# The attention heads' products in three rounded terms, x loaded a second time, and an opening by three queues

## The chip, the core and the metric

The kernel runs on one core of one Trainium2 chip. A core has five engines with instruction streams of their own: TensorE (PE in the profile, its weight loads PEld), VectorE (DVE), ScalarE (ACT), GpSimd (POOL) and SyncE (SP). DMAs are issued on the queues of SP, ACT and Pool and carried by the core's 16 DMA engines. The metric is the time of one execution on the device in microseconds (us), the median of several runs.

## The reference

One layer of a streaming encoder, all in float32, with S = 256 rows, D = 2048 columns, 16 heads of 128 columns:

```python
h = rms_norm(x, attn_norm)
proj = h @ w_in                      # 2048 x 6152: qa, ka, va, fa, qb, kb, vb
# group A, 8 heads, forgetting attention
qa, ka = rms_norm(heads(qa), q_norm), rms_norm(heads(ka), k_norm)
c = cumsum(log_sigmoid(fa + b_forget))
p = softmax(qa . ka / sqrt(128) + c[t] - c[s], s <= t);        out_a = p @ va
# group B, 8 heads, stick-breaking attention
z = qb . kb / sqrt(128)
log_beta = log_sigmoid(z);  log_1m = where(s < t, log_beta - z, 0)
suffix = reverse_cumsum(log_1m) - log_1m
w = where(s < t, exp(log_beta + suffix), 0);                   out_b = w @ vb
x = x + concat(rms_norm(out_a, out_norm_fox), rms_norm(out_b, out_norm_sb)) @ w_out
# feed-forward: causal convolution of width 3, gate, down projection
u = conv(rms_norm(x, ffn_norm) @ w_up) + conv_b                # 2048 x 11264
x = x + (silu(gate) * val) @ w_down                            # 5632 x 2048
```

## The kernel before

**Numbers in two parts.** The weights come from memory as F32. Each block of weights (a tile `w_raw`, mostly 1 MB) is split into two tiles of the rounded type F32R: ScalarE casts it to `w_hi` (L197), VectorE subtracts to get the rest, `w_lo` (L198). The activations (`hT`, `oT`) are kept in two such parts as well. A large product is then three F32R products that add up in PSUM: high by high, high by low, low by high. `in_three` (L219) does that for `token_major` products with 512 columns; `from_features` (L246, L253) does it where features lie on the partitions, with 512 columns for the high part of the weights and 256 for the low part.

**Order.** The opening (the first projection, one block of q) and the feed-forward part are ordered by hand (`tc.manual_schedule`). Between them a scheduler orders every engine's instructions by priority and dependency. The blocks of weights are loaded on SP's queue and split with a high priority, two blocks ahead (`whi` and `wlo` have two buffers each, `wraw` three). The work of the heads is written as generators, which wait in a queue (`waiting`); after each step of a projection (24 products of 512 columns, or 32 products in `from_features`) `step()` advances the first two of them. PE thus does a head's small products at the boundaries between two steps, and DVE and ACT do what lies between those products while PE works on the next step.

**The heads.** Heads of group A (`fox_head`): the rows of q and k are normed (`fox_rows`) and transposed (`to_heads`) into F32 tiles `qA`, `kA`; `ps_s` holds the scores of 128 and 256 columns (L505, L506), DVE and ACT make the softmax `pr`, PE transposes it (L530), ACT copies it to `pT`, and `ps_o` is the product with `vA` (L536, L537). Heads of group B (`sb_head`): q and k come as features on partitions from `sb_heads`, `ps_z` holds the scores (L576, L577); ACT makes Abs, Exp and Ln, DVE the softplus `sp`, both split it into `sps`, PE adds the sums over the later keys with six F32R products against `ntri` (L595 to L597), ACT takes Exp to get `w`, DVE limits it, and `ps_o` is the product with `vB` (L604, L605). All score products and value products are plain F32 products; the `ntri` products are F32R. `attended` scales the result into `oT` (L331, high and low part) and sums its squares.

**The opening.** `opening()` loads slices of x and of `w_in`, transposes x with the identity (first 128 columns of `cs`), scales it with the columns of `prow` (`attn_norm`) into `hT` (ACT, L140, then DVE's low part, L143), and multiplies (L386). SP's queue starts with x and then `cs`, ACT's with the first half of the first weights, then `prow`, then the second half:

```python
load_x(0, 2)
nc.sync.dma_start(cs[:, :P], cst[:, :P])
load_w(0, nc.scalar, [0])
nc.scalar.dma_start(prow[:KT, :], attn_norm[0].rearrange("(n p) -> n p", p=P))
load_w(0, nc.scalar, [1])
...
keep_busy(17)
columns(ga, prow[:KT, :], KT)
keep_busy(0)
split_w(0)
keep_busy(6)
```

`keep_busy(n)` is n products of a tile of zeros, whose result nobody uses; Pool sets the zeros (L344).

**x and minus_c.** x stays in the tile `x2` (2 MB) from the opening to the output projection, which adds to it (L642). `minus_c`, the gates of group A spread over all partitions, is made through a small tensor in memory, `c_rows`, on Pool's queue.

Of the kernel before, what the change touches and what calls it, by code (L numbers as in the profile page):

```python
# [8 lines left out]
F32 = mybir.dt.float32  # L9
# [5 lines left out]
P = 128  # L15
# [26 lines left out]
def hybrid_layer(  # L42
# [39 lines left out]
    x2 = big.tile([P, NT, D], F32, name="x2")  # L82
# [191 lines left out]
    with ExitStack() as actx:  # L274
# [15 lines left out]
        def to_heads(dst, rows, t, scale):  # L290

            ps = psb.tile([P, 4, P], F32, name="ps_h", tag="t")
            for h in range(4):
                nc.tensor.transpose(ps[:, h, :], rows[:, h * HD : (h + 1) * HD], ident)  # L294
            act.activation(dst[:, :, t * P : (t + 1) * P], ps, AF.Identity, scale=scale)
# [30 lines left out]
        def attended(po, h, g, group):  # L326

            o = oT[group * NH + h]
            act.activation(o[:, 0, :], po, AF.Identity, scale=g[:, h : h + 1])
            dve.scalar_tensor_tensor(  # L330
                o[:, 1, :], po, g[:, h : h + 1], f32(o[:, 0, :]), op0=ALU.mult, op1=ALU.subtract  # L331
            )
            if h == 0:
                act.activation(ssq[group], po, AF.Square)
            else:
                sq = tmp.tile([P, S], F32, name="osq", tag="t1", bufs=3)
                act.activation(sq, po, AF.Square)
                dve.tensor_tensor(ssq[group], ssq[group], sq, op=ALU.add)
# [5 lines left out]
        nc.gpsimd.memset(zeros, 0.0)  # L344
# [8 lines left out]
        def opening():  # L353
# [14 lines left out]
            def split_w(c):  # L368
                hi = whi.tile([P, 2048], F32R, name="w_hi", tag="w_hi")
                lo = wlo.tile([P, 2048], F32R, name="w_lo", tag="w_lo")  # L370
                parts.append([t[:, :1024].rearrange("p (a b) -> p a b", a=2) for t in (hi, lo)])
                for i, n in pairs[c]:
                    cols = slice(i * 512, (i + n) * 512)
                    act.copy(hi[:, cols], raws[c][:, cols])
# [71 lines left out]

        def heads_tile(name):
            return at.tile([P, 4, S], F32, name=name, tag="qk", bufs=4)

        qT0 = heads_tile("qA0")  # L450
# [3 lines left out]
        vA = at.tile([P, NT, WF], F32, name="vA")  # L454
        lf = at.tile([P, NT, NH], F32, name="lf")
        for j in range(3):
            acc = project(2 * WF + 344 * j, 344)
            n = 344 if j < 2 else 336
            for t in range(NT):
                scaled(vA[:, t, 344 * j : 344 * j + n], acc[:, t, :n], t)  # L460
                if j == 2:
                    dve.scalar_tensor_tensor(
                        lf[:, t, :], acc[:, t, 336:344], rstd1[:, t : t + 1], bf,
                        op0=ALU.mult, op1=ALU.add,
                    )


        c_of = at.tile([P, NT, NH], F32, name="c_of")
        minus_c = at.tile([P, NH, S], F32, name="minus_c")
# [3 lines left out]
        def gates():  # L473
# [19 lines left out]
            nc.gpsimd.dma_start(minus_c, c_rows.unsqueeze(0).to_broadcast([P, NH, S]))  # L493

        waiting.append(gates())
        step()

        def fox_head(h, qT, kT, first):
# [4 lines left out]
            q, k = qT[:, h % 4, :], kT[:, h % 4, :]  # L503
            s0, s1 = ps[:, 0, :], ps[:, 1:3, :].rearrange("p a b -> p (a b)")
            nc.tensor.matmul(s0, q[:, :P], k[:, :P], start=True, stop=False)  # L505
            nc.tensor.matmul(s1, q[:, P:], k, start=False, stop=True)  # L506
# [3 lines left out]
            for o, s, t in ((p0, s0, 0), (p1, s1, 1)):  # L510
                dve.scalar_tensor_tensor(
                    o, minus_c[:, h, : (t + 1) * P], c_of[:, t, h : h + 1], s, op0=ALU.add, op1=ALU.add
                )
# [17 lines left out]
            pT = tmp.tile([P, 3, P], F32, name="pT", tag="pT")  # L531
            act.copy(pT, pt)
            yield
            po = psb.tile([P, S], F32, name="ps_o", tag="t")
            hs = slice(h * HD, (h + 1) * HD)
            nc.tensor.matmul(po, vA[:, 0, hs], pT[:, 0:2, :].rearrange("p a b -> p (a b)"), start=True, stop=False)  # L536
            nc.tensor.matmul(po[:, P:], vA[:, 1, hs], pT[:, 2, :], start=False, stop=True)  # L537
            attended(po, h, g_fox, 0)

        for half in range(2):  # L540
            if half:
                qT = heads_tile("qA1")
# [4 lines left out]
            kT = heads_tile(f"kA{half}")  # L547
# [12 lines left out]
        def sb_heads(c0, scale, name):  # L560
            dst = heads_tile(name)
# [6 lines left out]
            return dst  # L568

        def sb_head(h, qT, kT, v):  # L570
            q, k = qT[:, h % 4, :], kT[:, h % 4, :]
# [4 lines left out]
            mm(z0, k[:, :P], q, start=True, stop=False)  # L576
            mm(z1, k[:, P:], q[:, P:], start=False, stop=True)  # L577
# [20 lines left out]
            w = tmp.tile([P, 3, P], F32, name="w", tag="pT")  # L598
            act.activation(w, ps, AF.Exp)
            dve.tensor_tensor(w[:, 0::2, :], w[:, 0::2, :], limit2, op=ALU.min)  # L600
            yield
            po = psb.tile([P, S], F32, name="ps_o", tag="t")
            hs = slice((h % 4) * HD, (h % 4 + 1) * HD)
            mm(po, v[:, 0, hs], w[:, 0:2, :].rearrange("p a b -> p (a b)"), start=True, stop=False)  # L604
            mm(po[:, P:], v[:, 1, hs], w[:, 2, :], start=False, stop=True)  # L605
            attended(po, h, g_sb, 1)

        for half in range(2):
            qT = sb_heads(B0 + 512 * half, R1q, f"qB{half}")
            kT = sb_heads(B0 + WF + 512 * half, R1, f"kB{half}")  # L610
            v = at.tile([P, NT, 512], F32, name=f"vB{half}", tag="vB", bufs=1)
            acc = project(B0 + 2 * WF + 512 * half, 512)
            for t in range(NT):
                scaled(v[:, t, :], acc[:, t, :], t)
# [11 lines left out]
        for group in range(2):  # L626
# [378 lines left out]
```

## Time and profile before

| | |
|---|---|
| median of 3 runs | 1116.93 us (1116.54 to 1117.72) |
| profiled execution, its own time | 1115.63 us |
| span of its instructions | 1113.7 us |
| busy PE (products) | 1106.9 us, 99% |
| busy PEld (weight loads) | 957.9 us, 86% |
| busy DVE | 862.7 us, 77% |
| busy ACT | 692.7 us, 62% |
| busy POOL | 27.2 us, 2% |
| TensorE's granted clock | 1.00 over the whole span |
| DMA | 231.34 MB, mean 208 GB/s |

Busy times are of each engine alone, so they overlap. Weight loads lie beside the products: a product's weights are loaded while the one before is under way. A row of the chain names the work that the last instruction can be followed back to. In rows of single instructions or groups of neighbours, the first two numbers are start and length in us, then engine, line, operation, output <- inputs, shape and count, and in brackets idle time before it and what ended that.

### The profile page before, as it was taken

The page shows a single profiled execution, that of the slowest core. Times are in us where ns is not written, and L with a number is a line of the kernel's source. Part 1 is how long each engine was busy: PE and PEld are TensorE (multiplying, and loading weights), DVE is VectorE, ACT ScalarE, POOL GpSimd, SP SyncE. Part 2 cuts the span into 40 slices and gives each one's busy share as a digit, 9 for nine tenths or more (in the row PEclk, how much of TensorE's full clock was granted, in tenths as well). Part 3 has the DMA queues.
Part 4 walks back from the last instruction along what each step waited for, and adds up shares of the span by engine and source line. Part 5 has one row for each costly group of instructions (what it writes and reads, how often), then busy time and mean ns, then how long its engine had stood idle before and what let it go on. Part 6 is the DMA issues. An engine that isn't in the chain of part 4 may idle for free.

```text
span 1113.7 us, 14715 instructions
## 1 busy us (share of the span) xinstructions
PE 1106.9 (99%) x5873; PEld 957.9 (86%) x5873; DVE 862.7 (77%) x906; ACT 692.7 (62%) x849; POOL 27.2 (2%) x27
## 2 busy tenths in 40 slices
PE   9999999999999999999999999999999999999998
PEld 7998888888888888888888888888888888888886
DVE  5745666657666677788899898989989899989973
ACT  6544545355565567666777767775777667776751
POOL 0000000000000000000000000000000000000000
PEclk9999999999999999999999999999999999999999
DMA  8676656564445486496869696788859697697941
GB/s 260 213 227 227 190 152 189 155 185 153 152 152 164 137 271 207 126 263 181 259 211 254 208 265 218 227 243 228 248 184 251 219 266 248 193 266 195 297 161 67
DMA packets 172479, 231.34 MB, mean 208 GB/s; under 512 B 4192, under 2 KB 118266, under 8 KB 172282
## 3 DMA queue, kind: packets, MB, share of 16 engines
q1 hardware_dynamic: 162378, 209.93, 58.3%
q0 software_dynamic: 9712, 19.93, 10.2%
q8 instruction: 46, 0.75, 0.3%
q10 hardware_dynamic: 320, 0.53, 0.2%
q14 instruction: 23, 0.19, 0.0%
HBM read 228.28 MB, written 2.11 MB: 207 GB/s over the span
## 4 chain that ended last, share of the span: by engine, by line
PE 98%; DVE 1%; DMA 0%; ACT 0%; issue 0%; SPq 0%; DVEq 0%; ACTq 0%
PE pu L246 33%; PE acc L219 24%; PE pu L253 18%; PE bank_a L219 10%; PE bank_b L219 4%; PE bank_c L219 2%; PE acc L386 2%; PE ps_x L135 1%; DVE w_lo L198 1%; DMA cs<-in_cst_dram 0%; PE ps_z L576 0%; PE ps_o L604 0%; PE ps_s L506 0%; PE ps_o L536 0%; PE ps_h L294 0%; PE ps_p L530 0%
## 5 line engine op out<-in xcount | busy, mean ns | idle before, releaser
L198 DVE TENSOR_TENSOR w_lo<-w_raw,w_hi 128x2048 fp32r<-128x2048 f32 (+2 forms) x200 | 440.1, 2204 | 161.9 <-ACT w_hi L197 156.0
L197 ACT CAST w_hi<-w_raw 128x2048 fp32r<-128x2048 f32 (+2 forms) x200 | 368.1, 1841 | 239.4 <-PE acc L219 91.2
L246 PE MATMUL pu<-hT,w_hi 128*128 128x512 f32 x1664 | 397.6, 391 | 0.0
L246 PEld LDWEIGHTS pu<-hT,w_hi 128*128 128x128 f32 x1664 | 310.1, 188 | 63.2
L253 PEld LDWEIGHTS pu<-hT,w_lo 128*128 128x128 f32 x1664 | 213.6, 191 | 8.2
L253 PE MATMUL pu<-hT,w_lo 128*128 128x256 f32 x1664 | 216.2, 283 | 0.0
L219 PE MATMUL acc<-w_hi,hT 128*128 128x512 f32 (+1 forms) x576 | 126.0, 370 | 0.0
L219 PEld LDWEIGHTS acc<-w_hi,hT 128*128 128x128 f32 x576 | 101.6, 188 | 14.3
L709 ACT ACTIVATE tap<-up,ccol 128x256 f32<-128x256 f32 x176 | 74.6, 495 | 0.0
L198 DVE TENSOR_TENSOR w_lo<-w_sum,w_hi 128x2048 fp32r<-128x2048 f32 (+1 forms) x30 | 62.2, 2073 | 13.4 <-ACT w_hi L197 10.6
L197 ACT CAST w_hi<-w_sum 128x2048 fp32r<-128x2048 f32 (+1 forms) x30 | 51.9, 1731 | 22.8 <-PE pu L246 22.8
L219 PE MATMUL acc<-w_lo,hT 128*128 128x512 f32 (+1 forms) x288 | 64.6, 366 | 0.0
L219 PEld LDWEIGHTS acc<-w_lo,hT 128*128 128x128 f32 x288 | 51.6, 188 | 7.5
L219 PE MATMUL acc<-w_hi,oT 128*128 128x512 f32 x192 | 46.3, 393 | 0.0
L219 PE MATMUL bank_a<-w_hi,g 128*128 128x512 f32 x176 | 44.2, 392 | 0.0
L219 PEld LDWEIGHTS acc<-w_hi,oT 128*128 128x128 f32 x192 | 35.4, 188 | 7.0
L219 PEld LDWEIGHTS bank_a<-w_hi,g 128*128 128x128 f32 x176 | 31.8, 189 | 5.7
L219 PE MATMUL bank_a<-w_hi,s 128*128 128x512 f32 x144 | 36.5, 393 | 0.0
L219 PE MATMUL bank_b<-w_hi,s 128*128 128x512 f32 x144 | 36.4, 392 | 0.0
L714 DVE TENSOR_TENSOR gate<-gate,tap 128x512 f32<-128x512 f32 x44 | 30.3, 688 | 2.3
L714 DVE TENSOR_TENSOR val<-val,tap 128x512 f32<-128x512 f32 x44 | 30.3, 688 | 2.3
L815 POOL DMA_DIRECT2D w_raw<-in_w_down_dram x10 | 12.7, 1270 | 779.6 <-DVE s L761 373.9
(176 smaller groups left out, 1052.1 us busy)
## 6 DMA issues: line engine op xcount, KB each, us to landing
w_raw<-in_w_up_dram SPq DMA_DIRECT2D x88, 1024.0 KB, 5.8
w_raw<-in_w_down_dram SPq DMA_DIRECT2D x40, 1024.0 KB, 5.3
w_raw<-in_w_in_dram SPq DMA_DIRECT2D x36, 1024.0 KB, 5.3
w_raw<-in_w_out_dram SPq DMA_DIRECT2D x16, 1024.0 KB, 5.2
w_raw<-in_w_in_dram SPq DMA_DIRECT2D x12, 688.0 KB, 4.2
w_raw<-in_w_down_dram POOLq DMA_DIRECT2D x8, 1024.0 KB, 12.0
w_sum<-in_w_down_dram POOLq DMA_DIRECT2D x8, 1024.0 KB, 9.0
w_raw<-in_w_down_dram SPq DMA_DIRECT2D x8, 512.0 KB, 4.0
```

The lines of the kernel that those rows point to most:

```text
L135: nc.tensor.transpose(ps[:, j, t * P : (t + 1) * P], xt[t][:, (k + j) * P : (k + j + 1) * P], ident)
L197: act.copy(hi[:, :n], raw[:, :n])
L198: dve.tensor_tensor(lo[:, :n], raw[:, :n], f32(hi[:, :n]), op=ALU.subtract)
L219: nc.tensor.matmul(o, lhs(i, l, t), r[:, i, :], start=starts and j == 0, stop=stops and j == 3 * n - 1, skip_group_check=more,)
L246: nc.tensor.matmul(acc[:, j, :], hi[:, i, j * P : (j + 1) * P], hT[:, k].rearrange("p a b -> p (a b)"), start=k == 0, stop=False,)
L253: nc.tensor.matmul(acc[:, j, S:], lo[:, i, j * P : (j + 1) * P], hT[:, k, 0, :], start=False, stop=k == KT - 1,)
L386: nc.tensor.matmul(acc[:, t, :], of_half(hT[:, 2 * c + i + j], l, t), r[:, j, :], start=high and c == i == m == 0, stop=not high and c == ...
L709: act.activation(taps[w][:, j, :], u[:, j, w : w + S], AF.Copy, scale=ccol[:, w, f : f + 1])
L714: dve.tensor_tensor(a, a, tap, op=ALU.add)
L815: nc.gpsimd.dma_start(mem[into][:, : nk * 512].rearrange("p (a b) -> p a b", a=nk), src, accum_op=ALU.add)
```

## The change

- Group A and B keep q, k, v, `pT` and `w` as F32R high and low parts, and each F32 product of the heads becomes three F32R products (`of_parts`): high by high, high by low, low by high. ACT writes the high parts, DVE the low parts.
- The low parts need room. Those of q and k (group A, and the first half of group B) lie in a tile `low` in the place of `x2`; those of group B's second half lie in two buffers of the tag `raw`; `vA_low` lies where `oT` of the first four heads of group B comes later; `vB0_low` lies in the place of the first half of `minus_c`, which becomes two tiles and two loads; `vB1` has both parts in the place of `vA`.
- x is therefore loaded a second time, by two DMAs of 1 MB on Pool's queue, at the first step of the output projection, once all of group A and the first four heads of group B have their scores. Its first use there is L642 before, L705 after.
- In the opening, Pool's queue loads `cs` and `prow`, SP's and ACT's queues one row block of x each and then one half of the first weights each; DVE makes the first `w_hi` cast in place of ACT, and sets the zeros in place of Pool; `keep_busy` makes 16 and 5 products for 17 and 6.
- `attended` squares on ACT ahead of DVE's low part, for all heads in the same way.

```diff
-    x2 = big.tile([P, NT, D], F32, name="x2")
+    x2 = big.tile([P, NT, D], F32, name="x2", tag="x2")
 ...
             for h in range(4):
                 nc.tensor.transpose(ps[:, h, :], rows[:, h * HD : (h + 1) * HD], ident)
-            act.activation(dst[:, :, t * P : (t + 1) * P], ps, AF.Identity, scale=scale)
+            hi, lo = (part[:, :, t * P : (t + 1) * P] for part in dst)
+            act.activation(hi, ps, AF.Identity, scale=scale)
+            dve.scalar_tensor_tensor(lo, ps, scale, f32(hi), op0=ALU.mult, op1=ALU.subtract)
 ...
-        oT = [late.tile([P, 2, S], F32R, name=f"oT{h}") for h in range(2 * NH - 4)]
-        oT += [hT[:, KT - 4 + i] for i in range(4)]
+        oT = [late.tile([P, 2, S], F32R, name=f"oT{h}") for h in range(NH)]
+        vA_low = late.tile([P, NT, WF], F32R, name="vA_low", tag="oT_sb")
 ...
-        nc.gpsimd.memset(zeros, 0.0)
+        dve.memset(zeros, 0.0)
 ...
-                    act.copy(hi[:, cols], raws[c][:, cols])
                     if c == i == 0:
+                        dve.tensor_copy(hi[:, cols], raws[c][:, cols])
                         transposed_split(0, ga)
+                    else:
+                        act.copy(hi[:, cols], raws[c][:, cols])
 ...
-            load_x(0, 2)
-            nc.sync.dma_start(cs[:, :P], cst[:, :P])
-            load_w(0, nc.scalar, [0])
-            nc.scalar.dma_start(prow[:KT, :], attn_norm[0].rearrange("(n p) -> n p", p=P))
+            nc.gpsimd.dma_start(cs[:, :P], cst[:, :P])
+            nc.gpsimd.dma_start(prow[:KT, :], attn_norm[0].rearrange("(n p) -> n p", p=P))
+            for t, queue in enumerate((nc.sync, nc.scalar)):
+                queue.dma_start(xt[t][:, : 2 * P], xf[t * P : (t + 1) * P, : 2 * P])
+            load_w(0, nc.sync, [0])
             load_w(0, nc.scalar, [1])
 ...
-            keep_busy(17)
+            keep_busy(16)
             columns(ga, prow[:KT, :], KT)
-            keep_busy(0)
             split_w(0)
-            keep_busy(6)
+            keep_busy(5)
 ...
+        low = big.tile([P, 4, 4, S], F32R, name="low", tag="x2")
+
+        def of_parts(o, a, b, start, stop):
+            for i, (j, k) in enumerate(((0, 0), (0, 1), (1, 0))):
+                nc.tensor.matmul(o, a[j], b[k], start=start and i == 0, stop=stop and i == 2)
+
+        def values(dst, acc):
+            hi, lo = dst
+            for t in range(NT):
+                scaled(hi[:, t, :], acc[:, t, :], t)
+            for t in range(NT):
+                dve.scalar_tensor_tensor(
+                    lo[:, t, :], acc[:, t, :], rstd1[:, t : t + 1], f32(hi[:, t, :]),
+                    op0=ALU.mult, op1=ALU.subtract,
+                )
 ...
+        def weighted(v, hs, w):
+            po = psb.tile([P, S], F32, name="ps_o", tag="t")
+            wp = [w[:, i].rearrange("p a b -> p (a b)") for i in range(2)]
+            of_parts(po, [part[:, 0, hs] for part in v], [p[:, :S] for p in wp], True, False)
+            of_parts(po[:, P:], [part[:, 1, hs] for part in v], [p[:, S:] for p in wp], False, True)
+            return po
 ...
-            pT = tmp.tile([P, 3, P], F32, name="pT", tag="pT")
-            act.copy(pT, pt)
+            pT = tmp.tile([P, 2, 3, P], F32R, name="pT", tag="pT")
+            act.copy(pT[:, 0], pt)
+            dve.tensor_tensor(pT[:, 1], pt, f32(pT[:, 0]), op=ALU.subtract)
 ...
                 t2 = summed(tmp, acc, "t2", bufs=1)
-                dve.tensor_tensor(
-                    dst[:, i : i + 2, :], t2, scale.unsqueeze(1).to_broadcast([P, 2, S]), op=ALU.mult
-                )
+                dve.tensor_tensor(t2, t2, scale.unsqueeze(1).to_broadcast([P, 2, S]), op=ALU.mult)
+                act.copy(hi, t2)
+                dve.tensor_tensor(lo, t2, f32(hi), op=ALU.subtract)
 ...
-            mm(z0, k[:, :P], q, start=True, stop=False)
-            mm(z1, k[:, P:], q[:, P:], start=False, stop=True)
+            of_parts(z0, [part[:, :P] for part in k], q, True, False)
+            of_parts(z1, [part[:, P:] for part in k], [part[:, P:] for part in q], False, True)
 ...
-            w = tmp.tile([P, 3, P], F32, name="w", tag="pT")
-            act.activation(w, ps, AF.Exp)
-            dve.tensor_tensor(w[:, 0::2, :], w[:, 0::2, :], limit2, op=ALU.min)
+            e = tmp.tile([P, 3, P], F32, name="e", tag="pr")
+            act.activation(e, ps, AF.Exp)
+            dve.tensor_tensor(e[:, 0::2, :], e[:, 0::2, :], limit2, op=ALU.min)
+            w = tmp.tile([P, 2, 3, P], F32R, name="w", tag="pT")
+            act.copy(w[:, 0], e)
+            dve.tensor_tensor(w[:, 1], e, f32(w[:, 0]), op=ALU.subtract)
 ...
                 acc = token_major(lambda k: oT[group * NH + k], wo, group * NH, NH, 512 * c, 512)
+                if group == c == 0:
+                    assert scored[: NH + 4] == list(range(NH + 4))
+                    x2 = big.tile([P, NT, D], F32, name="x2", tag="x2")
+                    xt[:] = [x2[:, t, :] for t in range(NT)]
+                    for t in range(NT):
+                        nc.gpsimd.dma_start(xt[t], xf[t * P : (t + 1) * P, :])
```

More of the change, by code (lines that the diff above doesn't have):

```diff
@@ L465, in hybrid_layer @@
                     )
+            values([part[:, :, 344 * j : 344 * j + n] for part in vA], acc[:, :, :n])
         c_of = at.tile([P, NT, NH], F32, name="c_of")
-        minus_c = at.tile([P, NH, S], F32, name="minus_c")
+        minus_c = [at.tile([P, 4, S], F32, name=f"minus_c{i}", tag=f"minus_c{i}") for i in range(2)]
         dram = actx.enter_context(tc.tile_pool(name="dram", bufs=1, space=bass.MemoryType.DRAM))
@@ L492, in gates @@
             nc.gpsimd.dma_start(c_rows, mine[:NH])
-            nc.gpsimd.dma_start(minus_c, c_rows.unsqueeze(0).to_broadcast([P, NH, S]))
+            for i in range(2):
+                rows = c_rows[4 * i : 4 * i + 4, :]
+                nc.gpsimd.dma_start(minus_c[i], rows.unsqueeze(0).to_broadcast([P, 4, S]))
         waiting.append(gates())
         step()
+        def weighted(v, hs, w):
[4 more added lines that the diff above has]
+            return po
         def fox_head(h, qT, kT, first):
@@ L502, in fox_head @@
             ps = pss.tile([P, 3, P], F32, name="ps_s", tag="s")
[L503 removed]
+            q, k = ([part[:, h % 4, :] for part in parts] for parts in (qT, kT))
             s0, s1 = ps[:, 0, :], ps[:, 1:3, :].rearrange("p a b -> p (a b)")
[L505 to L506 removed]
+            of_parts(s0, [part[:, :P] for part in q], [part[:, :P] for part in k], True, False)
+            of_parts(s1, [part[:, P:] for part in q], k, False, True)
+            scored.append(h)
             pr = tmp.tile([P, 3, P], F32, name="pr", tag="pr")
```

76 lines of the change are left out of this document (45 added, 31 removed).

## The prediction

> **What bounds the kernel now.** I read the page's first part (busy time), its fourth part (the chain that ended last), then a table by stage, then TensorE's weight loads one by one around the heads, then the first 11 us.
>
> ```profile
> span 1113.7 us, 14715 instructions
> PE 1106.9 (99%) x5873; PEld 957.9 (86%) x5873; DVE 862.7 (77%) x906; ACT 692.7 (62%) x849; POOL 27.2 (2%) x27
> PE 98%; DVE 1%; DMA 0%; ACT 0%; issue 0%; SPq 0%; DVEq 0%; ACTq 0%
> 202.00:303.00 101.00, 101.00 (x540) 87.40 (x539) 62.94 (x85) 54.08 (x75) 0.00 (x0) 1.00 0.54 167
> ```
>
> PE is busy 99% of the span and is 98% of the chain. In the stage of the heads (last row: stretch, its length, busy PE, PEld, DVE, ACT, POOL, clock, DMA share, GB/s) PE has no gap, at clock 1.00, while DVE works 63 and ACT 54 of 101 us. So the change is worth what it does to PE's own work and to the first microseconds, before PE has work, and it costs what new waits it puts before PE. The profiled execution took 1115.63 us for a span of 1113.7; the median of the runs shown is 1116.93, 1.30 more. I add my sum to both.
>
> **1. The products of the heads.** Each of 16 heads has one pair of score products and one pair of value products, each pair 256 and 128 columns wide, in F32 (L505/L506, L576/L577; L536/L537, L604/L605). After the change each is three F32R products (`of_parts`): 32 groups of 2 F32 products become 32 groups of 6 F32R products. The trace of before holds both kinds: the `ntri` products (L595 to L597) are six F32R products of 256 and 128 columns. Weight loads (start, length):
>
> ```profile
> 275.88 3.52 PEld L219 LDWEIGHTS acc<-w_hi,hT 128*128 128x128 f32 x16
> ...
> 282.03 0.19 PEld L595 LDWEIGHTS ps_z<-sps,masksR 128*128 128x128 f32 x1
> ...
> 282.60 0.19 PEld L597 LDWEIGHTS ps_z<-sps,masksR 128*128 128x128 f32 x1
> 282.71 3.49 PEld L219 LDWEIGHTS acc<-w_hi,hT 128*128 128x128 f32 x16
> ...
> 288.05 0.42 PEld L604 LDWEIGHTS ps_o<-w,vB 128*128 128x128 f32 x2
> ...
> 288.83 0.30 PEld L576 LDWEIGHTS ps_z<-qB,kB 128*128 128x128 f32 x2
> ...
> 289.48 3.48 PEld L219 LDWEIGHTS acc<-w_hi,hT 128*128 128x128 f32 x16
> ...
> 294.82 0.19 PEld L595 LDWEIGHTS ps_z<-sps,masksR 128*128 128x128 f32 x1
> ...
> 295.61 0.30 PEld L576 LDWEIGHTS ps_z<-qB,kB 128*128 128x128 f32 x2
> ...
> 296.26 3.51 PEld L219 LDWEIGHTS acc<-w_hi,hT 128*128 128x128 f32 x16
> ```
>
> And from the chain in order of time:
>
> ```profile
> 350.66 16.34 PE acc L219 x72
> 426.79 3.65 PE pu L246 x16
> 430.44 1.91 PE pu L253 x16
> ```
>
> A projection step is 24 products of 512 columns: 16.34/72 x 24 = 5.447 us (0.227 each). From one step's first weight load to the next's is that plus the head work between. 282.71 to 289.48 is 6.77 with two F32 pairs in it: 1.32, so 0.66 a pair. 289.48 to 296.26 is 6.78 with six `ntri` products and one F32 pair: 1.33, less 0.66 gives 0.67. 275.88 to 282.71 is 6.83, with the same two kinds: 1.38, less 0.66 gives 0.72. So six `ntri` products cost 0.67 to 0.72. Their six loads start evenly, from 282.03 to 282.60 in five steps: 0.114 each, though four of them have only 128 columns. A 256-column product costs 1.91/16 = 0.120 (L253). The `ntri` six are then 2 x 0.120 + 4 x 0.114 = 0.70, as found. A new group is 3 x 0.120 + 3 x 0.114 = 0.70 against 0.66: +0.04, times 32 = **+1.3 us**. Bounds: 0.68 and 0.73 for the group (the two readings of `ntri`, plus 0.012 for two more wide products), so +0.7 to +2.3. That a 128-column F32R product costs as much as half an F32 pair, which would be several us more, is excluded by the loads' even 0.114.
>
> The rule that speaks for a gain is in the Trainium skill, TensorE: Matmul & The Clock Gate, "Back-to-back issue gap": an isolated product takes N/2.4 + 2.5 ns, 56 ns for 128 columns and 109 for 256, by which a group would be 0.49 us and all 32 would save 5 us. The same page's "LDWEIGHTS (loading the stationary operand)" gives 128/1.2 = 107 ns for a weight load; the trace's 114 ns agrees with this one and not with the gap.
>
> **2. The opening.** Before, SP issues x and then `cs` (identity), ACT the first weights and `prow`. After, Pool issues `cs` and `prow`, SP and ACT half of x each and then half of the first weights each; DVE makes the first `w_hi` cast instead of ACT, and the `zeros` memset instead of Pool. `keep_busy` gives up two idle products, which lie in PE's wait. Behind Pool's two loads nothing stands until `c_rows`, in the stage of the heads.
>
> ```profile
> 0.74 0.44 SPq L87 DMA_DIRECT2D x<-in_x_dram  x1
> 1.23 4.08 DMA cs<-in_cst_dram
> 4.74 0.62 ACT L374 CAST w_hi<-w_raw 128x512 fp32r<-128x512 f32 x1 [1.24 <-DMA w_raw<-in_w_in_dram]
> 5.42 0.13 PEld L125 LDWEIGHTS pp<-cs,prow 16*128 16x128 f32 x1 [1.25 <-DMA prow<-in_attn_norm_dram]
> 6.28 0.84 ACT L140 ACTIVATE hT<-ps_x,ga 128x256 fp32r<-128x256 f32 x2 [0.92 <-PE ps_x L135]
> 6.80 1.61 PE L386 MATMUL acc<-w_hi,hT 128*128 128x512 f32 x4
> 7.15 0.87 DVE L143 SCALAR_TENSOR_TENSOR hT<-ps_x,ga,hT 128x256 fp32r<-128x256 f32 x2 [1.28 <-ACT hT L140]
> 10.99 2.10 PE L386 MATMUL acc<-w_hi,hT 128*128 128x512 f32 x8
> 2.00:3.00 1.00, 1.00 (x7) 0.69 (x6) 0.00 (x0) 0.78 (x1) 0.00 (x0) 1.00 0.95 161
> 3.00:4.00 1.00, 1.00 (x7) 0.74 (x6) 0.00 (x0) 0.50 (x1) 0.00 (x0) 1.00 0.94 297
> 4.00:5.00 1.00, 0.45 (x5) 0.15 (x2) 0.00 (x0) 0.26 (x1) 0.00 (x0) 1.00 1.12 368
> c_rows<-mine POOLq DMA_DIRECT2D x1, 8.0 KB, 1.8
> minus_c<-c_rows POOLq DMA_DIRECT2D x1, 1024.0 KB, 7.0
> L439 DVE CAST masksR<-masks x1: 418/418/418, 35.4 to 35.4; 128x512 fp32r<-128x512 f32 x1
> ```
>
> The end of `cs` at 5.31 starts everything: PE transposes, ACT's `hT` at 6.28, first product at 6.80, DVE's low parts at 7.15, and a steady rhythm from 10.99. The product needs x 0.26 MB, `cs` 0.07, `prow` 0.01, first weights 0.26: 0.60 MB. The rows by microsecond move 0.16 + 0.30 + 0.37 MB from 2.00 to 5.00, so 0.60 MB are through at about 4.4 and 0.86 MB (with the other half of the first weights) at about 5.1. `cs` from Pool, first on its queue and so issued at about 0.74 as SP's first is now: between 1.8 us (8 KB) and 7.0 us (1 MB) on that queue; at 64 KB I take the first plus the 0.2 us its bytes need, so about 3, and `prow` within 1 us after. Then the first weights are last: between 4.4 and 5.1, then 0.42 us for DVE's cast (the `masksR` row, same shape): first product at 5.2 to 5.6, against 6.80. DVE's low parts follow its cast at once, 1 us or more sooner than 7.15, and ACT's next cast has lost the one ahead of it. The bytes of the later slices set a limit too: DMA stands at 0.94 to 1.12 of its engines. I take **-1.0 us**; from -1.6 (everything moves by 6.80 less 5.2) to nothing.
>
> **3. The low parts.** New on DVE: a subtraction a head for `pT` and `w` (128x384), one for every 512-column block of q, k and v; new on ACT: a cast for `w` and for the stick-breaking q and k. All PE's operands, so their cover is the time until PE's next boundary between two steps, where it uses them. The tightest is the stick-breaking chain, where ACT's order after the change puts the `w` cast between Exp and Ln of the next head, and DVE's puts the `w` low part ahead of `sp`:
>
> ```profile
> 297.65 0.52 ACT L582 ACTIVATE e<-e 128x384 f32<-128x384 f32 x1
> 299.26 0.51 ACT L589 CAST sps<-sp 128x384 fp32r<-128x384 f32 x1 [1.08 <-DVE sp L587]
> 297.58 0.42 DVE L600 TENSOR_TENSOR w<-w,masksR 128x256 f32<-128x256 f32 x1
> 299.80 0.56 DVE L590 TENSOR_TENSOR sps<-sp,sps 128x384 fp32r<-128x384 f32 x1 [0.58 <-ACT sps L589]
> 301.62 0.42 PEld L604 LDWEIGHTS ps_o<-w,vB 128*128 128x128 f32 x2
> 302.40 0.19 PEld L595 LDWEIGHTS ps_z<-sps,masksR 128*128 128x128 f32 x1
> 320.41 0.75 DVE L642 SCALAR_TENSOR_TENSOR x<-acc,rg,x 128x512 f32<-128x512 f32 x1
> ```
>
> DVE ends `sps` at 300.36, PE takes it at 302.40: 2.0 us of cover. Ahead of it come ACT's wait for DVE's `w` min (298.00 less 297.65, 0.35), the cast (0.51) and, if DVE cannot place it beside ACT's Ln, the subtraction (0.56): 1.4 us at most. So **nothing**, with 0.6 us to spare. The splits of the next weights have a whole step more of cover, since two buffers hold them. One place has no cover:
>
> ```profile
> PE ps_h L294 <- DVE rs_u L112: 0.2, 1, 0.2
> ```
>
> There PE waits already for DVE to scale the rows of k; low parts of q that stand in front of it in DVE's new order can add the 0.3 us that PE's next transposes leave. I keep that for the range.
>
> **4. x a second time.** `low` takes x's place, so Pool loads 2 MB of x once the fourth stick-breaking head has its scores (295.61 and what follows), and DVE's first use is at 320.41 (L642, L705 after): 24 us. If it lands late, DVE stands before L705 with the low part of `sps` and the next split queued behind, and PE waits for them one boundary later. The nearest rows on Pool's queue, with weights loading beside them:
>
> ```profile
> w_raw<-in_w_down_dram POOLq DMA_DIRECT2D x8, 1024.0 KB, 12.0
> ```
>
> Twice 1 MB: 12 us side by side, 24 end to end. The first is nearest, since the stage's DMA share is 0.54. **Nothing**; the end-to-end reading would just reach its use.
>
> Sum: 1.3 - 1.0 + 0 + 0 = +0.3. Against the profiled 1115.63 that is 1115.9, against the median **1117.2 us**. Under 0.2% (2.2 us), about what a measurement of this kernel can tell from no change.
>
> **The rivals.** *The chain at the boundaries is late* (slower). Place: part 3. It decides once ACT and DVE lose over 2.0 us between a head's scores and its `sps`. Against it: the 1.4 worked out. For it: that is one step of many, and ACT's split of the next weights may fall into the chain where a projection copies too. An overshoot of 0.5 us at the boundary of each of 8 heads is +4.0: 1121.2.
>
> *Narrow products at their column rate* (faster): the 0.114 belongs to `ntri` and not to every 128-column F32R product. From 0.227 at 512 and 0.120 at 256 columns, 128 would be 0.067; a group 0.56, 32 groups -3.2, with the opening 1112.7. Against it: 0.114 in every `ntri` row above; no other F32R product of 128 columns is in the trace.
>
> *Three queues only save issue time*: the first product still waits for the same bytes, and `cs` goes out at 0.74 instead of 1.23: -0.5, sum +0.8, 1117.7. For it: DMA share 0.94 from 2.00 on. Against it: `cs` ended at 5.31, when by 5.00 over 0.8 MB were through, more than the product needs. This is the rule of the Trainium skill, DMA: Bandwidth & Descriptors, "Issuing engines are not separate DMA queues": all run on the same 16 engines, and several issuers only save the sequencer's time.
>
> *Pool's queue is late at the start*: `cs` after 7.0 us lands at 7.7, 2.4 later than now, and the product with it: 2.4 + 1.3 = +3.7, 1120.6.
>
> **How the numbers follow.** Forecast 0.47, late chain 0.16, column rate 0.12, issue time 0.20, Pool late 0.05. Faster by over 0.2%: column rate and the edge of the forecast, 0.14. Slower: late chain, Pool late and a little edge, 0.22. Within: 0.64. The range goes from the near side of the column rate, 1114.0, to the near side of the late chain, 1120.6; beyond lie about 0.1 on each side. The forecast's own is 1116.0 (+0.7 - 1.6) to 1119.5 (+2.3 + 0 + 0.3 for the place without cover).
>
> **What would show it.** Right: between two steps' first loads 6.81 to 6.87 where 6.77 to 6.83 stood; the first product before 6.0; PE without gaps from 30 to 410 us; DVE at L705 without a wait for x. Wrong: loads of the new products closer than 0.1 us; PE or PEld waiting for `sps`, `w` or `pT`; `cs` landing after 5.3; PE waiting anywhere for DVE behind x.

## The result, and the profile after

The changed kernel takes 1118.80 us (median of 16 runs, 1118.35 to 1122.02), and the kernel before, run beside it, 1115.78 us (16 runs). The ratio is 1.0029, with a 95% interval from 1.0022 to 1.0035: slower by 3.0 us, where the forecast was +0.3. (The kernel before took 1115.78 here, 1.15 less than the median of three runs that the forecast was added to, so the forecast is compared as a change.) The profiled execution took 1118.61 us for a span of 1116.8, 3.1 more than before.

The page of the changed kernel, its chain, and the stage of the heads (columns as before):

```profile
span 1116.8 us, 14941 instructions
PE 1109.3 (99%) x5935; PEld 961.6 (86%) x5935; DVE 885.5 (79%) x950; ACT 697.2 (62%) x864; POOL 29.2 (3%) x31
PE 98%; DVE 1%; DMA 0%; issue 0%; POOL 0%; ACT 0%; DVEq 0%; POOLq 0%
202.00:303.00 101.00, 101.00 (x568) 88.28 (x567) 72.15 (x101) 57.15 (x84) 1.05 (x2) 1.00 0.54 167
```

In the heads' stage PE still has no gap, with DVE 9 us busier than before. So neither the low parts nor the second load of x put a wait before PE. All that PE waited for, by the table of waits of the changed kernel, lies in the opening:

```profile
PE pp L125 <- DMA prow<-in_attn_norm_dram: 2.1, 1, 2.1
PE idle L355 <- DVE zeros L350: 1.1, 1, 1.1
```

Where the 3.1 us arise is read from weight loads that both kernels have. The kernel before, start and length: the second projection begins, the gates are done, the heads are done.

```profile
32.76 2.61 PEld L219 LDWEIGHTS acc<-w_hi,hT 128*128 128x128 f32 x16
96.92 3.59 PEld L219 LDWEIGHTS acc<-w_hi,hT 128*128 128x128 f32 x16
361.17 3.59 PEld L219 LDWEIGHTS acc<-w_hi,hT 128*128 128x128 f32 x16
```

The same loads of the changed kernel:

```profile
35.28 2.61 PEld L219 LDWEIGHTS acc<-w_hi,hT 128*128 128x128 f32 x16
99.19 3.59 PEld L219 LDWEIGHTS acc<-w_hi,hT 128*128 128x128 f32 x16
364.47 3.59 PEld L219 LDWEIGHTS acc<-w_hi,hT 128*128 128x128 f32 x16
```

It is 2.52 us late after the opening, 2.27 after the gates, 3.30 after the heads, and 3.1 at the end. So the opening cost 2.5, the gates gave 0.25 back, and the heads cost 1.03.

The opening of the changed kernel, in order of time:

```profile
1.27 0.71 POOL L399 DMA_DIRECT2D cs<-in_cst_dram  x1 [0.83 <-POOLq L1053]
1.98 0.55 POOL L400 DMA_DIRECT2D prow<-in_attn_norm_dram  x1
1.06 3.60 PE L355 MATMUL idle<-zeros 128*128 128x256 bf16 x16 [1.06 <-DVE zeros L350]
6.72 0.20 PE L125 MATMUL pp<-cs,prow 16*128 16x16 f32 x1 [2.06 <-DMA prow<-in_attn_norm_dram]
6.85 0.65 PE L135 MATMUL ps_x<-cs,x 128*128 128x128 f32 x4
7.34 0.71 PE L355 MATMUL idle<-zeros 128*128 128x256 bf16 x5
8.07 2.11 PE L394 MATMUL acc<-w_hi,hT 128*128 128x512 f32 x4
```

And its chain, where the load of `prow` stands with issue and length:

```profile
1.98 4.60 DMA prow<-in_attn_norm_dram
```

Pool issues `cs` at 1.27, not at 0.74, takes 0.71 us for it, and issues `prow` behind it. `prow` lands at 6.58, `cs` after 4.3 us at 5.57. PE ends its idle products at 4.66, pauses 2.06 us, and the first product comes at 8.07 instead of 6.80: 1.27 late. The other 1.25 of the 2.52 come behind it. In the stretches of the changed kernel, the third number from the right is the granted clock:

```profile
8.40:8.60 0.20, 0.20 (x2) 0.00 (x0) 0.18 (x1) 0.20 (x1) 0.00 (x0) 0.64 1.06 410
8.60:8.80 0.20, 0.20 (x1) 0.00 (x0) 0.20 (x1) 0.20 (x1) 0.00 (x0) 0.50 1.03 399
11.60:11.80 0.20, 0.20 (x2) 0.11 (x1) 0.00 (x0) 0.20 (x2) 0.00 (x0) 0.50 1.00 123
11.80:12.00 0.20, 0.20 (x2) 0.17 (x1) 0.06 (x1) 0.20 (x2) 0.00 (x0) 0.83 0.69 92
```

The clock is halved from about 8.46 (0.64 over 0.20 us is 0.06 at full and 0.14 at half) to about 11.87 (0.83), 3.41 us. Four `w_hi` products take 2.11 us there, 1.61 before.

The heads, weight loads of the changed kernel:

```profile
278.58 3.52 PEld L219 LDWEIGHTS acc<-w_hi,hT 128*128 128x128 f32 x16
285.45 3.48 PEld L219 LDWEIGHTS acc<-w_hi,hT 128*128 128x128 f32 x16
...
291.61 0.19 PEld L465 LDWEIGHTS ps_z<-qB,kB 128*128 128x128 f32 x1
...
292.18 0.19 PEld L465 LDWEIGHTS ps_z<-qB,low 128*128 128x128 f32 x1
292.29 3.50 PEld L219 LDWEIGHTS acc<-w_hi,hT 128*128 128x128 f32 x16
299.13 3.49 PEld L219 LDWEIGHTS acc<-w_hi,hT 128*128 128x128 f32 x16
...
305.29 0.19 PEld L645 LDWEIGHTS ps_z<-sps,masksR 128*128 128x128 f32 x1
```

From step to step it is 6.87, 6.84 and 6.84, where 6.83, 6.77 and 6.78 stood. The six loads of a new group start evenly: 291.61 to 292.18 in five steps, 0.114 each.

### The profile page after: what moved, and what is told of

Its sections match the earlier page's. It is cut to its first block, busy times and chain, and to the rows that moved or that the text cites. A ratio compares the mean times of both kernels' runs of the same rounds, so it can differ in the third digit from the quotient of the medians.

```text
span 1116.8 us, 14941 instructions
## 1 busy us (share of the span) xinstructions
PE 1109.3 (99%) x5935; PEld 961.6 (86%) x5935; DVE 885.5 (79%) x950; ACT 697.2 (62%) x864; POOL 29.2 (3%) x31
## 3 DMA queue, kind: packets, MB, share of 16 engines
HBM read 230.37 MB, written 2.11 MB: 208 GB/s over the span
## 4 chain that ended last, share of the span: by engine, by line
PE 98%; DVE 1%; DMA 0%; issue 0%; POOL 0%; ACT 0%; DVEq 0%; POOLq 0%
PE pu L246 34%; PE acc L219 24%; PE pu L253 18%; PE bank_a L219 10%; PE bank_b L219 4%; PE bank_c L219 2%; PE acc L394 2%; PE ps_o L465 1%; PE ps_x L135 1%; PE ps_s L465 0%; PE ps_z L465 0%; DMA prow<-in_attn_norm_dram 0%; PE ps_h L294 0%; PE ps_p L571 0%; PE ps_z L645 0%
## 5 line engine op out<-in xcount | busy, mean ns | idle before, releaser
L758 DVE TENSOR_TENSOR up<-t,R 128x512 f32<-128x512 f32 x44 | 30.4, 692 | 1.5
L855 DVE TENSOR_TENSOR x<-x,bank_a 128x512 f32<-128x512 f32 (+1 forms) x43 | 28.6, 668 | 3.5 <-PE bank_a L219 3.5
L219 PE MATMUL acc<-w_hi,oT 128*128 128x512 f32 x128 | 31.0, 394 | 0.0
```

The source lines that it names most:

```text
L219: nc.tensor.matmul(o, lhs(i, l, t), r[:, i, :], start=starts and j == 0, stop=stops and j == 3 * n - 1, skip_group_check=more,)
L758: dve.tensor_tensor(u[:, :, 2:], t2, R, op=ALU.mult)
L855: dve.tensor_tensor(xs, xs, ps[:, i : i + n], op=op)
```

## The experiments

My theory after the comparison: of the 3.1 us, the opening cost 2.5 (half through `prow`'s late landing, half through the clock behind PE's pause), the heads' products 1.0, and 0.25 came back at the gates. The rivals: the low parts on DVE and ACT cost, and the opening is absorbed later; narrow products at their column rate; three loaded queues rather than `prow`'s place. Each experiment was timed against the kernel before on the same chip. The table holds how much later than in the kernel before four weight loads start in the profiled execution (the first product's at 6.80, and those at 32.76, 96.92 and 361.17), and the ratio; the sixth experiment is told by itself. The first kernel has the opening of before and yet its first product comes 0.19 earlier, so differences of 0.2 us between single executions mean little.

| kernel | first product | second projection | after the gates | after the heads | ratio (95%) |
|---|---|---|---|---|---|
| changed | +1.27 | +2.52 | +2.27 | +3.30 | 1.0029 (1.0022 to 1.0035) |
| 1 heads alone | -0.19 | -0.18 | -0.44 | +0.63 | 1.0005 (0.9996 to 1.0014) |
| 2 opening alone | +1.97 | +2.01 | +2.02 | +2.02 | 1.0021 (1.0012 to 1.0030) |
| 3 more idle products | +1.39 | +1.39 | +1.50 | +2.57 | 1.0018 (1.0010 to 1.0027) |
| 4 `prow` on ACT's queue | +0.62 | +0.85 | +0.62 | +1.65 | 1.0010 (1.0001 to 1.0019) |
| 5 before, fewer idle products | +0.59 | +0.89 | +0.88 | +0.89 | 1.0006 (0.9997 to 1.0015) |
| 7 before, `cs` and `prow` first | -0.23 | -0.23 | -0.25 | -0.24 | 0.9994 (0.9986 to 1.0003) |
| 8 before, x first | +0.70 | +0.21 | +0.18 | +0.22 | 0.9999 (0.9990 to 1.0008) |
| 9 changed, `cs` and `prow` first | -0.35 | -0.34 | -0.24 | +0.80 | 0.9999 (0.9990 to 1.0008) |
| 10 as 7, 14 idle products | -0.36 | -0.29 | -0.31 | -0.30 | 0.9992 (0.9983 to 1.0000) |

**1. The heads' part alone.** The changed kernel with the opening of before: its loads, ACT's first cast, Pool's zeros, 17 and 6 idle products.

```diff
-            nc.gpsimd.dma_start(cs[:, :P], cst[:, :P])
-            nc.gpsimd.dma_start(prow[:KT, :], ...)
+            load_x(0, 2)
+            nc.sync.dma_start(cs[:, :P], cst[:, :P])
+            load_w(0, nc.scalar, [0])
+            nc.scalar.dma_start(prow[:KT, :], ...)
```

> The changed kernel with the opening of before. Theory (late opening): of the 3.1 us by which the span grew, 2.5 came from the opening, 1.0 from the heads' products, and 0.2 went back at the gates. So the first product at 6.8 us, clock 1.00 throughout, 0.8 us over before (ratio 1.0007). Rival (low parts): the wait of DVE and ACT at the boundaries is what cost, and the opening's delay is absorbed later: then this kernel stays 2 us or more over before (ratio 1.002 or more). Rival (narrow products at their column rate): faster than before by 3 us.

Measured: first product at 6.61, ratio 1.0005. From the gates to the end of the heads it loses 1.07 us, and the span is 0.3 over before. The interval of the ratio reaches down to no change, so the 1.07 rests on the trace. Theory kept; low parts as the main cost are out, and so is a gain from narrow products.

**2. The opening alone.** The kernel before with the changed kernel's loads, cast, zeros and 16 and 5 idle products.

> The kernel before with only the new opening (Pool's queue for cs and prow, halves of x on SP and ACT, DVE's first cast and zeros, 16 and 5 idle products). Theory (late opening): first product near 8.1, clock halved for about 3.4 us after it, +2.5 us against before (ratio 1.0022). Rival (the cover of 24 us of later weights absorbs it, and the cost lies in the heads): under +0.7 us.

Measured: +2.0 us from the first product on, and nothing of it absorbed to the end of the heads; ratio 1.0021. The two parts add up: 1.0005 and 1.0021 against 1.0029. But the place of the slow clock is another. PE in this kernel:

```profile
6.83 0.26 PE L125 MATMUL pp<-cs,prow 16*128 16x16 f32 x1 [2.17 <-DMA prow<-in_attn_norm_dram]
7.01 1.11 PE L135 MATMUL ps_x<-cs,x 128*128 128x128 f32 x4
7.92 1.27 PE L349 MATMUL idle<-zeros 128*128 128x256 bf16 x5
8.85 1.65 PE L388 MATMUL acc<-w_hi,hT 128*128 128x512 f32 x4
```

Four transposes take 1.11 us (0.65 in the changed kernel) and five idle products 1.27 (0.71), so the slow stretch lies ahead of the first product here: that comes 0.7 us later still (its weight load at 8.77), and the products after it lose nothing more. And it is of another kind. Every profiled execution begins at the slow pace and comes to the faster one at a moment of its own. In the kernel before that is within the first idle products:

```profile
2.78 1.06 PE L349 MATMUL idle<-zeros 128*128 128x256 bf16 x4
3.96 0.49 PE L349 MATMUL idle<-zeros 128*128 128x256 bf16 x3
```

A row ends with its last product, 0.42 us long in the first and 0.27 in the second; without it the products start 0.21 and then 0.11 us apart. The changed kernel's 16 are all 0.21 apart, its five behind the pause 0.11, and at 8.46 the pace falls back. In the second experiment's kernel it has not risen before the first product. So a fall-back behind PE's pause is what the changed kernel's profiled execution shows; this one shows a pace that rose late.

**3. More idle products.** The changed kernel with:

```diff
-            keep_busy(16)
+            keep_busy(24)
```

> The changed kernel with 24 idle products ahead of the first transposes in place of 16; each takes about 0.22 us, so PE's pause from 4.66 to 6.72 us shrinks to about 0.3. Theory (two costs, late prow and the halved clock behind PE's pause): the first product still near 8.1, but the clock stays at 1.00, and 1.2 us come back: +1.9 us against before (ratio 1.0017), where the changed kernel has +3.1. Rival (the clock is halved for another reason, the DMA load or the start of the real products): clock still 0.5 from 8.5 to 11.9, and no gain. Rival (the halved clock costs nothing, since PE waits for ACT and DVE there): clock 1.00, no gain.

Measured: the pause is 0.47 us, the first product comes at 8.19, and the products behind it keep their pace:

```profile
6.83 0.20 PE L125 MATMUL pp<-cs,prow 16*128 16x16 f32 x1 [0.47 <-DMA prow<-in_attn_norm_dram]
6.97 0.66 PE L135 MATMUL ps_x<-cs,x 128*128 128x128 f32 x4
8.19 0.73 PE L394 MATMUL acc<-w_hi,hT 128*128 128x512 f32 x2
```

At the second projection it is 1.39 late and no longer 2.52: the halved clock was worth 1.13, with `prow` as late as ever. The intervals of this kernel and the changed one overlap, so the 1.13 rests on the traces. The mean granted clock that is on record for each run adds to it: 3.41 us at half are 1.7 us lost of 1116.8, and make it 0.998. So it stands in 10 of the changed kernel's 16 runs and in 4 of the second's 10, but in none of this kernel's 11, and in no run of any other kernel here, 80 runs of the kernel before among them. The changed kernel's other six runs were no faster (1118.35 to 1122.02 us, against 1118.45 to 1119.32); that the pace rose late in them, as in the second's profile, would explain it and is not shown. A third of the 1.13 (0.35) goes again at 47 us, where PE's transposes of q now wait 0.5 us for DVE's scaled rows.

**4. `prow` on ACT's queue.** The changed kernel with:

```diff
-            nc.gpsimd.dma_start(prow[:KT, :], ...)
+            nc.scalar.dma_start(prow[:KT, :], ...)
```

> The changed kernel with prow as the first load on ACT's queue; cs stays on Pool's. Theory (prow is late because it stands second on Pool's queue): cs still lands near 5.6, prow before it, the first transposes start near 5.7 and the first product near 7.0; PE's pause is about 1.0 us and the clock stays at 1.00. +1.1 us against before (ratio 1.0010). Rival (the DMA engines are loaded by the three queues, and whatever is needed last lands at about 6.6): first product still near 8.0, +3 us. Rival (x now lands last, being second on ACT's queue): first product between 7.2 and 7.8, +1.5 us.

Measured: ratio 1.0010, and PE stops waiting at 5.45, for `cs` from Pool (4.1 us after its issue). That `prow` was late by its place is kept, and the interval lies below the changed kernel's. The first product came at 7.42, not 7.0, since the clock part was wrong for this execution: its four transposes took 1.12 us and the five idle products behind them 1.27. That is the slow pace of the second experiment: as there, it had not risen yet (the first 16 took 3.59). The rival of a late x is out, because the transposes followed `pp` at once.

**5. Fewer idle products, all loads as before.** The kernel before with:

```diff
-            keep_busy(17)
+            keep_busy(10)
```

> The kernel before with 10 idle products at the start in place of 17: they end near 3.2 us, and PE pauses about 2.2 us until cs and prow are there at about 5.4, as long as in the changed kernel, with every load as before. Theory (the pause itself costs clock): first product still near 6.8, but products at half rate somewhere in the microseconds behind it, +1.2 us against before (ratio 1.0011). Rival (the late prow brings both costs, and a pause without it none): ratio 1.000, products at the pace of before.

Measured: `pp` at 5.22, when the loads are there, but the first product at 7.39:

```profile
1.10 2.31 PE L349 MATMUL idle<-zeros 128*128 128x256 bf16 x10 [1.10 <-POOL zeros L344]
5.22 0.26 PE L125 MATMUL pp<-cs,prow 16*128 16x16 f32 x1 [1.81 <-DMA cs<-in_cst_dram]
5.41 1.12 PE L135 MATMUL ps_x<-cs,x 128*128 128x128 f32 x4
7.46 1.94 PE L386 MATMUL acc<-w_hi,hT 128*128 128x512 f32 x4
```

The slow products stand ahead of the first real product and at it, not only behind, and cost 0.89 us in the trace, where I expected 1.2. The ten idle products were as slow (0.21 apart), so PE had no faster pace to lose in its pause: with fewer idle products, and no load late, the pace rose later in this execution. That a pause by itself sets the pace back is not shown by this run. Its ratio of 1.0006 has an interval that reaches down to no change: the trace shows the 0.89, the times alone don't.

**6. One term for the narrow products.** The first experiment's kernel, with the corrections of the heads' 128-column products (high by low, low by high) left out, 64 products:

```diff
+            terms = ((0, 0), (0, 1), (1, 0)) if b[0].shape[-1] > P else ((0, 0),)
```

> The heads' part alone with the opening of before (as the first experiment), but the 128-column products of the heads keep only high by high: the two corrections of each are left out, 32 x 2 = 64 products. Theory (a 128-column product costs the pitch of its weight load, 0.114): 7.3 us less than the first experiment, -6.5 against before (ratio 0.9942). Rival (they cost their columns, 0.067): 4.3 us less, -3.5 against before (ratio 0.9969). Rival (DVE and ACT set the pace at the boundaries): less than 2 us.

Measured: ratio 0.9964 (0.9951 to 0.9976), -4.0 us, near the column rate's forecast; but the loads speak against it. Two steps of group A of this kernel:

```profile
125.16 3.51 PEld L219 LDWEIGHTS acc<-w_hi,hT 128*128 128x128 f32 x16
131.09 3.51 PEld L219 LDWEIGHTS acc<-w_hi,hT 128*128 128x128 f32 x16
```

and of the first experiment's:

```profile
125.47 3.51 PEld L219 LDWEIGHTS acc<-w_hi,hT 128*128 128x128 f32 x16
131.62 3.51 PEld L219 LDWEIGHTS acc<-w_hi,hT 128*128 128x128 f32 x16
```

5.93 against 6.15 with two products fewer: 0.11 each, the pitch of the weight loads. That the total falls short of 64 x 0.114 = 7.3, and that the interval leaves out the -6.5 forecast, has another reason, as far as the trace tells: later in the heads the scheduler placed the `ntri` products inside the steps, and PE's weight loads then waited for their operands, as the table of waits shows:

```profile
PEld ps_z L644 <- ACT sps L638: 1.2, 3, 0.6
PEld ps_z L644 <- DVE sps L639: 1.1, 3, 0.4
```

The first experiment's table has no such rows. So the price holds where the order is the same, and the boundary chain that was my slower rival does bind once the order leaves it less room. How much of the shortfall these waits make is not shown.

**7 and 8. Two other openings for the kernel before.** Without Pool's queue, with halves of x on SP and ACT, and DVE's first cast. The seventh starts with `cs` on SP and `prow` on ACT; the eighth has x first.

```diff
+            nc.sync.dma_start(cs[:, :P], cst[:, :P])
+            nc.scalar.dma_start(prow[:KT, :], ...)
             for t, queue in enumerate((nc.sync, nc.scalar)):
                 queue.dma_start(xt[t][:, : 2 * P], ...)
+            load_w(0, nc.sync, [0])
```

> The kernel before (F32 heads) with another opening: cs first on SP's queue and prow first on ACT's, then one half of x on each, then one half of the first weights on each; DVE makes the first cast; 17 and 6 idle products. Theory (what is small and needed is first, and lands first): cs and prow land by 4.9, x by 5.4, first product near 6.5, 0.3 us under before (ratio 0.9997), clock as before. Rival (each load's latency of 4 to 5 us is set by its place in a queue, so x, now second, lands at 6 or later): first product at 7.2 or later, +0.4 us or more, and more still where the pause costs clock.

> As the kernel that puts cs and prow first, but with the halves of x first on SP's and ACT's queues and cs and prow second: the change's use of these two queues without Pool's. Theory: cs and prow are issued at about 1.2 and land near 5.2 as before, x by 5.0, first product between 6.5 and 6.8: 0 to 0.3 us under before (ratio 0.9997 to 1.000). Rival (three queues were needed, because the second place on a busy queue lands past 6): first product past 7.3, +0.5 us or more.

Measured: the seventh has its first product at 6.57 and stays 0.24 ahead to the end of the heads, as expected, though that is hardly more than the 0.19 between two executions of one opening. In the eighth x, `cs` and `prow` come in time too, but the first product comes at 7.50: PE waits 1.0 us for DVE's first `w_hi`. Its weights were issued at 1.65 in both kernels but came late in this one (the half on ACT's queue landed 5.5 us after its issue, 4.1 in the seventh). The rival's time, past 7.3, came, but by the weights and not by `cs` or `prow`, and with one profile of each the cause stays open; from the second projection on only 0.2 us of it are left.

The seventh's span is 1114.6, 0.9 over before, although it is ahead after the heads. Its table of waits has a row that the kernel before and the changed kernel lack, at 665.9 us in the feed-forward part:

```profile
PE bank_a L219 <- DVE x L795: 1.1, 1, 1.1
```

The profiled executions of the second, fifth and tenth have it too, at other places (0.9, 0.3 and 0.8 us). Why it comes in some executions stays open; runs of the kernel before differ by more than that (1115.03 to 1118.60), so a span says little about an opening, and the table stops at the heads.

**9. The changed kernel with that opening.**

> The changed kernel with cs first on SP's queue and prow first on ACT's, then the halves of x and of the first weights, and 17 and 6 idle products: nothing on Pool's queue. Theory (the opening's loss is the two loads on Pool's queue and PE's pause behind them; the heads cost 1.0 and the gates give 0.2 back): first product near 6.6, +0.6 us against before (ratio 1.0005). Rival (something else of the changed kernel, such as DVE's first cast or the low parts, keeps part of the loss): +1.5 us or more.

Measured: 1116.32 us, ratio 0.9999 (0.9990 to 1.0008). By the trace it is 0.35 ahead at the first product; the transposes of q take that back as in the third experiment, here at 45 us; the gates give 0.24, the heads cost 1.04, and it ends the heads 0.80 late. The intervals of this kernel and the changed one don't meet: the opening's loss goes with Pool's two loads and the pause behind them, and DVE's first cast, which this kernel keeps, takes no part in it.

**10. The seventh with 14 idle products.**

> The kernel before (F32 heads) with cs and prow first as in the seventh experiment, and 14 idle products in place of 17: there the first transposes stood behind the idle products until 4.84. Theory (queue order on PE): the transposes start when cs and prow land, at 4.5 to 4.8, and the first product comes 0 to 0.3 us sooner than the 6.57 of that kernel; 0.3 to 0.5 us under before (ratio 0.9996). Rival (a shorter stretch of idle products leaves the clock at half rate for longer): first product at 7 or later in some executions, +0.5 us or more.

Measured: 1115.36 us, ratio 0.9992 (0.9983 to 1.0000). `pp` starts at 4.20 behind the idle products and waits for no load, earlier than I thought `cs` and `prow` would land; the slower pace that the rival named is there as well (four transposes in 1.12 us, six idle products in 1.49 against 0.82 in the seventh), and the first product is at 6.44. The best version is this or the seventh; both are faster than the changed kernel, and that either beats the kernel before is not shown by their intervals.

## Why the prediction was right or wrong

The time lies in the range, but the likeliest case, no change that can be measured, did not come: one term of its sum had the wrong sign. As a change, the forecast's own part went from -0.9 to +2.6 and does not hold the +3.0; the range does, to +3.7, because it ran up to the near side of a late chain that did not come. So its place in the range is luck, with one term right.

- **Heads' products, +1.3 forecast: +1.03 measured**, 0.032 for each of 32 groups where I had 0.04. The pitch of 0.114 for a 128-column F32R product held, in the changed kernel's loads and in the sixth experiment. The column-rate rival is out; the isolated gap of 56 ns that spoke for it (the Trainium skill, TensorE: Matmul & The Clock Gate, "Back-to-back issue gap") does not describe these products, each with a weight load of its own.
- **Opening, -1.0 forecast: +2.5 measured.** Two steps failed. "`cs` from Pool, first on its queue and so issued at about 0.74 ... about 3, and `prow` within 1 us after": it was issued at 1.27, and the loads took 4.3 and 4.6 us. The 8 KB row of `c_rows` (1.8 us), from a moment long behind the opening, was the wrong neighbour; the right one stood in the same fence, `cs` itself with 4.08 us on SP's queue. And "`keep_busy` gives up two idle products, which lie in PE's wait": I costed PE's wait at its length alone, without asking what it does to PE's pace, though the products of zeros stand there for no other visible use. The one product fewer ahead of the wait is about 0.2 us of its 2.06, and no run changed 17 to 16 alone; what made the wait long is `prow`. The fourth and ninth experiments confirm the first step by their times. The second rests on the third's trace and the granted clocks of the runs. The rival of a late Pool queue was the right one, at 0.05, though by `prow` instead of `cs`: its lateness is 1.27 where I priced 2.4, and it lacked the clock's 1.25.
- **Low parts, nothing forecast: nothing measured.** The tightest chain has its `sps` at 304.04 and PE takes it at 305.29 (rows below and above), so 1.25 us are left of 2.0, more than the 0.6 that I allowed, and PE and PEld wait for no `sps`, `w` or `pT`. The wait for `rs_u` that I feared would grow is not in the changed kernel's table.

```profile
303.48 0.56 DVE L640 TENSOR_TENSOR sps<-sp,sps 128x384 fp32r<-128x384 f32 x1 [0.58 <-ACT sps L639]
```

- **x a second time, nothing forecast: nothing measured.** Pool's two loads land within 7.8 us, and DVE uses x from 323.9:

```profile
L694 POOL DMA_DIRECT2D x<-in_x_dram x2: 527/528/530, 299.7 to 300.2; - x2
DMA to landing us min/median/max: 5.1/6.5/7.8
L705 DVE SCALAR_TENSOR_TENSOR x<-acc,rg,x x4: 740/749/751, 323.9 to 336.8; 128x512 f32<-128x512 f32 x4
```

- **The gates, not in the prediction: -0.25.** Before, PE's `pc` products stood in the middle of a step, with a weight load that sat idle for 0.36 us ahead of them; after, the scheduler puts them between two steps. The gain falls in the steps around them; that it comes of this was not tested. The kernel before and the changed kernel:

```profile
87.86 0.30 PEld L482 LDWEIGHTS pc<-lf,cs 128*128 128x128 f32 x2 [0.36 <-issue]
```

```profile
87.33 0.42 PEld L512 LDWEIGHTS pc<-lf,cs 128*128 128x128 f32 x2
```

The sum of what was found, 2.52 + 1.03 - 0.25, is the 3.30 after the heads; the 0.2 between that and the span's 3.1 I did not follow up.

## What to carry to other kernels

Take a load's time from a row of the same moment and not of the same size: at the start an 8 KB load took 4.6 us where 64 KB took 4.3. What is small and needed first goes first on a queue that issues early, and a queue that is free is no gain by itself. Count idle products that keep TensorE busy as work: before taking some out, or making a load behind them late, ask when PE's pace rises and whether a pause sets it back. And an F32 pair of products replaced by three F32R products each gained nothing here, because a 128-column product costs 0.114 us, hardly less than the 0.120 of a 256-column one.

## What the runs showed of the hardware

- PE's pace at the start. In every profiled execution the first idle products started 0.21 us apart, and later ones 0.11. The rise came within the first 17 in the kernel before (3.34 us for them), behind them in the seventh (3.81), and only behind the start of the first real product in the second, fourth, fifth and tenth. In the changed kernel it came by the end of the pause, and a stretch at half clock followed, 3.41 us long, which began 1.7 us after PE was busy again. The Trainium skill, TensorE: Matmul & The Clock Gate, "What's actually happening", tells of a window of 3413 ns that runs freely, so that the change of clock falls differently in each run. The length agrees with the 3.41 us here, and the moving place agrees as far as these few executions go; what sets the moment was not tested here.
- The column of the granted clock read 1.00 in places where products ran at half pace: the 16 idle products of the changed kernel took 3.60 us, 0.225 each, and the five after the pause 0.71, 0.14 each (0.21 and 0.11 apart). So does the 1.00 over the whole span of the kernel before, whose idle products are shown with the second experiment. In the first microseconds the durations of the products told more than that column.
